# fp32 scores of 64 rows, and a recurrence whose products all span 128 rows

## The chip, the cores and the metric

The kernel runs on one core of one Trainium2 chip. The metric is device time in microseconds: a run is timed from start to end, and the median of several runs counts. Beside that, one execution was recorded by the hardware profiler; all rows below come from it. Engines are named as the profile names them: PE is TensorE (products), PEld its weight loads, DVE VectorE, ACT ScalarE, POOL GpSimd, SP the engine whose queue issues the transfers.

## The reference

One inference step of a two-layer decoder: 1024 prompt tokens and 8 single-token samples, model width 1024. In each layer one input projection feeds three branches, whose gated results go through one output projection and are added to the layer's input.

- Pooling: trailing means over 2, 4, 8 or 16 tokens, and a small product per group.
- Attention: 8 query heads and 2 key heads of 64 channels, window 128, RMS norm and rotary on queries and keys, a learned sink in the softmax.
- RWKV-7: 4 heads, each with a 64 x 64 state that goes through the tokens one after another:

```python
def step(S, inp):
    r_t, w_t, k_t, v_t, kk_t, a_t = inp
    sa = jnp.einsum('bhvk,bhk->bhv', S, kk_t)
    S = S * w_t[:, :, None, :] - sa[..., None] * (kk_t * a_t)[:, :, None, :] + v_t[..., None] * k_t[:, :, None, :]
    o = jnp.einsum('bhvk,bhk->bhv', S, r_t)
    return S, o
```

Everything is float32.

## The kernel before, in words

Activations lie with channels on partitions and tokens on columns, in two halves (512 prompt tokens and the 8 samples; 512 prompt tokens). The large projections split each float32 operand into a high and a low part (type F32R) and add three products (high by high, high by low, low by high) into one PSUM tile `acc` of 128 x 512, 128 x 256 or 128 x 264. The weight's high part `wh` is cast on ScalarE and its low part `wl` on GpSimd or VectorE; three buffers of each are in turn.

Attention works in blocks of 128 queries and a pair of query heads (`attn_block`): 32 blocks in all, 16 of a layer. The block splits its queries into `qs` (ScalarE) and `ql` (VectorE, the tile QL); the keys `kh` hold high and low parts in the two halves of the partitions, so that two F32R products over 128 rows give one score tile of 128 x 256. `e` counts the key head, `j` the query head of the pair. Each `e` has a PSUM tile `ps` of its own. Then follow the softmax in `sm`, four transposes into `pt`, the copies `pcur` and `pall`, and the product with the values into `po`.

The recurrence is chunked: 32 tokens make a chunk, eight chunks a group (`g`), four groups a layer; 64 chunks in all, strictly in order. `rwkv_prep` prepares a group: decays (`cs`, `pin`, `pc`), the scaled keys BK, the scaled queries AG, their Gram products, and the inverse of a 32 x 32 triangle per chunk and head (X, transposed into TT). Then `values` and `flip` turn the values into XS and BK into BT through the PSUM tiles CA and CB. `rwkv_chain` does a chunk in three steps. The tile XS holds per chunk, pair `p` and head `e` of the pair the state (64 partitions), the corrected keys' rows (32) and the values (32). First, four products of XS with AG give `ys`; second, TT times `ys` gives the 32 correction rows of XS; third, BT times the lower or upper 64 rows of XS is added to the decayed state and becomes the state of the next chunk. The outputs of the chunk before (`osb`) are produced between the first and the second step.

The order on TensorE is written by a planner inside the kernel: every product has a planned cost (`mm`), every operation of another engine a planned end, and each branch is a generator that gives up its turn with `yield` of the tiles it needs next. The planner puts projection products between the steps of the branches, and a dependency without a semaphore fixes the order that results. Operations within `urgent()` get a higher priority in the queues of their engines. Both PSUM tiles for scores come from a ring of two (`att`).

All VectorE, ScalarE and GpSimd operations pass line 150 and all products line 308 of the kernel before, so the rows are told apart by their tiles.

## Time and profile before

| | |
|---|---|
| median of 3 runs | 1277.89 us (1267.9 to 1283.97) |
| the profiled execution | 1278.29 us, its span 1276.5 us |
| PE busy | 1107.7 us (87%) |
| DVE busy | 985.9 us (77%) |
| ACT busy | 642.0 us (50%) |
| POOL busy | 558.3 us (44%) |
| TensorE clock granted, mean | 0.934 |

The span runs from the first instruction to the last. A busy share is the time in which the engine had at least one instruction under way. The end of a product is modelled and products overlap; where the cost of products matters, the starts of their neighbours are compared. A product with float32 operands stands in the trace as two instructions, one with F32R operands as one (the column of shapes calls both f32). A row of waits says which engine and tile waited for which, how long in total, in how many places, and the longest.

### The profile page before, as it was taken

What the parts mean: (1) busy time and instruction counts of PE and PEld (TensorE: products, weight loads), DVE (VectorE), ACT (ScalarE), POOL (GpSimd) and SP (SyncE); (2) the same over time, 40 slices, a digit from 0 to 9 for tenths busy, and PEclk for the clock granted to TensorE, in tenths of its full rate; (3) what the DMA queues carried; (4) which work ended last, traced back from release to release, by engine and by line L of the source; (5) the groups of instructions that cost most, each with busy time, mean ns of one, the idle gap of its engine ahead of it and who ended that gap; (6) DMA issues with size and microseconds to landing.
All of it is one profiled execution on the core that took longest, in us unless ns stands there. A gap on an engine that the chain in (4) does not pass through costs nothing.

```text
span 1276.5 us, 24973 instructions
## 1 busy us (share of the span) xinstructions
PE 1107.7 (87%) x9258; PEld 889.1 (70%) x9258; DVE 985.9 (77%) x2193; ACT 642.0 (50%) x1651; POOL 558.3 (44%) x535
## 2 busy tenths in 40 slices
PE   7988788699898799989998879888998886899995
PEld 6987677476665568879887767665776664588664
DVE  6487997879769887897688997989447897878633
ACT  4265445544555564763464456555535545646421
POOL 3256544633454246441545544443454462344231
PEclk8998989798899799999999979999998997899997
DMA  6522223342221124334311212434242221244221
GB/s 186 160 81 69 87 55 101 103 135 76 59 89 59 34 84 154 114 113 123 121 53 61 78 56 79 149 128 137 82 134 68 64 75 44 74 150 130 65 74 68
DMA packets 81237, 120.37 MB, mean 94 GB/s; under 512 B 20430, under 2 KB 30174, under 8 KB 81116
## 3 DMA queue, kind: packets, MB, share of 16 engines
q1 hardware_dynamic: 81116, 118.79, 29.8%
q8 instruction: 72, 1.18, 0.4%
q14 instruction: 49, 0.40, 0.1%
HBM read 94.30 MB, written 19.17 MB: 89 GB/s over the span
## 4 chain that ended last, share of the span: by engine, by line
DVE 40%; PE 37%; issue 6%; ACT 5%; DMA 5%; POOL 4%; SPq 2%; POOLq 0%; DVEq 0%; ACTq 0%
PE acc L308 26%; DVE pr L150 4%; DVE AG L150 3%; PE CA L308 3%; DVE XS L150 3%; DVE sm L150 3%; DVE asm L150 3%; DVE ql L150 2%; DVE X L150 2%; PE po L308 2%; DMA sq<-z 2%; DVE hl L150 2%; SPq L160 2%; DVE z L150 1%; PE CB L308 1%
## 5 line engine op out<-in xcount | busy, mean ns | idle before, releaser
L308 PE MATMUL acc<-hh,wh 128*128 128x512 f32 (+2 forms) x1464 | 499.7, 342 | 11.7 <-ACT hh L150 5.1
L308 PE MATMUL acc<-hh,wl 128*128 128x512 f32 (+2 forms) x1464 | 492.9, 338 | 12.5 <-POOL wl L150 9.3
L308 PE MATMUL acc<-hl,wh 128*128 128x256 f32 (+3 forms) x1464 | 494.1, 338 | 4.6 <-DVE hl L150 4.6
L150 POOL TENSOR_TENSOR wl<-wst,wh 128x512 fp32r<-128x512 f32 (+1 forms) x223 | 307.8, 1383 | 348.3 <-ACT wh L150 285.0
L308 PEld LDWEIGHTS acc<-hh,wh 128*128 128x128 f32 x1464 | 285.8, 195 | 50.4 <-issue 9.1
L308 PEld LDWEIGHTS acc<-hh,wl 128*128 128x128 f32 x1464 | 284.6, 195 | 44.7 <-POOL wl L150 12.9
L308 PEld LDWEIGHTS acc<-hl,wh 128*128 128x128 f32 (+1 forms) x1464 | 283.6, 194 | 38.0 <-issue 7.9
L150 ACT CAST wh<-wst 128x512 fp32r<-128x512 f32 (+1 forms) x246 | 149.3, 609 | 166.6 <-PE acc L308 99.9
L150 ACT ACTIVATE sm<-sm,asm 128x128 f32<-128x128 f32 (+1 forms) x130 | 50.9, 393 | 39.2 <-DVE asm L150 37.0
L150 DVE TENSOR_TENSOR pr<-X,N 128x4 f32<-128x4 f32 (+15 forms) x128 | 65.4, 511 | 2.8 <-POOL ro L150 0.9
L150 ACT CAST qs<-q 64x256 fp32r<-64x256 f32 x128 | 51.9, 405 | 22.8 <-DVE q L150 10.6
L150 ACT ACTIVATE e<-e 128x520 f32<-128x520 f32 (+1 forms) x64 | 40.5, 634 | 35.3 <-DVE e L150 34.7
L150 DVE SCALAR_TENSOR_TENSOR XS<-XS,pc,CA 64x64 f32<-64x64 f32 x128 | 35.4, 277 | 20.2 <-PE CA L308 18.5
L150 DVE TENSOR_REDUCE X<-pr 128x2 f32<-128x4 f32 (+15 forms) x128 | 44.9, 351 | 2.0
L150 POOL TENSOR_TENSOR mx<-mx,e 128x520 f32<-128x520 f32 (+1 forms) x24 | 33.7, 1404 | 28.0 <-ACT e L150 28.0
L308 PE MATMUL ps<-kh,qs 128*128 128x256 f32 (+1 forms) x128 | 37.8, 316 | 8.2 <-ACT pall L150 3.4
L311 PE MATMUL pt<-cst,sm 128*128 128x128 f32 (+1 forms) x130 | 23.8, 311 | 23.2 <-DVE sm L150 15.3
L150 POOL TENSOR_TENSOR z<-z,rope 128x520 f32<-128x520 f32 (+1 forms) x20 | 31.9, 1595 | 26.1 <-DMA sq<-z 11.2
L150 DVE SCALAR_TENSOR_TENSOR xrkv<-xrkv,vec,zl 128x256 f32<-128x256 f32 x48 | 32.9, 734 | 13.0 <-POOL xrkv L150 13.0
L150 DVE TENSOR_TENSOR ql<-q,qs 64x256 fp32r<-64x256 f32 x64 | 40.5, 632 | 2.1 <-ACT qs L150 0.9
L308 PEld LDWEIGHTS CA<-XS,BT 64*64 64x64 f32 x256 | 13.1, 139 | 39.1 <-DVE XS L150 28.6
L150 ACT ACTIVATE sa<-sa 128x512 f32<-128x512 f32 (+2 forms) x56 | 28.3, 508 | 23.9 <-POOL sa L150 11.7
(258 smaller groups left out, 2109.6 us busy)
## 6 DMA issues: line engine op xcount, KB each, us to landing
wst<-in_w_in_dram SPq DMA_DIRECT2D x175, 256.0 KB, 2.7
wst<-in_w_out_dram SPq DMA_DIRECT2D x56, 256.0 KB, 2.8
zr<-ev SPq DMA_DIRECT2D x24, 256.0 KB, 3.0
zl<-zr SPq DMA_DIRECT2D x12, 385.5 KB, 3.5
sq<-z SPq DMA_DIRECT2D x40, 65.0 KB, 2.0
sq<-z SPq DMA_DIRECT2D x40, 64.0 KB, 2.0
xh<-in_x_dram SPq DMA_DIRECT2D x8, 260.0 KB, 5.6
xr<-in_x_dram SPq DMA_DIRECT2D x8, 260.0 KB, 2.8
```

What stands on the lines that cost most here:

```text
L150: return f(*a, **kw)
L160: return nc.sync.dma_start(out, in_)
L308: placed(T.matmul(out=out, lhsT=lhsT, rhs=rhs, start=start, stop=stop, **kw), n, out)
L311: placed(T.transpose(out=out, in_=in_, identity=identity), 300 if out.shape[0] > 64 else 130, out)
```

## The change

It has two large parts and some small ones.

Scores: queries and keys are no longer split. `kh` is one float32 tile; a block has four float32 products over the 64 partitions of their head, `e` the inner loop, instead of eight over 128. Both PSUM tiles are taken before the first of them.

Recurrence: BT, TZ (which replaces TT) and XS are filled so that every product of the chain runs over all 128 partitions. BT holds an identity where the state's rows lie, written once; TZ holds each 32 x 32 inverse in its own 32 partitions and zeros elsewhere. The keys are scaled to the end of the chunk instead of its start, so the state in XS is kept already times the chunk's decay; the third step's product then gives the new state whole, and one write per half multiplies it by the next chunk's decay (ScalarE for the upper 64 partitions, VectorE for the lower). All of the chain but the outputs now uses CA.

Small: constants are laid out anew, three masks as bytes; the products of BK with `pc` are gone, a subtraction on GpSimd precedes the exponentials; half of BT's copies go to VectorE; the planner's cost for a product of up to 64 rows and more than 64 output rows is lower.

```diff
     def load_cst():
+        for to, at, n in ((0, C_ID, 256), (K_MC, C_MC, 128), (K_REC, C_REC, 30), (K_TI, C_TI, 4)):
+            D.dma_start(cst[:, to:to + n], src[:, at:at + n])
...
+        G.tensor_copy(out=masks, in_=t[:, 0:384])
...
         def decays(p, sig):
-            tt(G, sig, cs, sig, ALU.subtract)
-            act(sig, sig, AF.Exp, scale=-CD)
             pin = t2("pin")
-            act(pin, cs, AF.Exp, scale=CD)
-            act(cs, cs, AF.Exp, scale=-CD)
-            S.copy(out=R.pc[:, p, :], in_=cs[:, 31:256:32])
+            tt(G, ch8(pin), ch8(cs), ch8(cs)[:, :, 31:32].to_broadcast([128, 8, 32]), ALU.subtract)
+            act(R.pc[:, p, :], cs[:, 31:256:32], AF.Exp, scale=-CD)
+            tt(G, sig, pin, sig, ALU.subtract)
+            act(cs, pin, AF.Exp, scale=-CD)
+            act(pin, pin, AF.Exp, scale=CD)
+            act(sig, sig, AF.Exp, scale=-CD)
...
-        for p in range(2):
-            tt(
-                G, BK[:, :, p].rearrange("p c x s -> p c (x s)"), BK[:, :, p].rearrange("p c x s -> p c (x s)"),
-                R.pc[:, p, :].unsqueeze(2).to_broadcast([128, 8, 64]), ALU.mult,
-            )
...
         values(0)
         values(1)
+        for h in range(4):
+            rows = slice(32 * h, 32 * h + 32)
+            V.transpose(
+                out=TZ[rows, :, h, :].rearrange("p c (i q) -> p i c q", q=4),
+                in_=X[rows].rearrange("p i (c q) -> p i c q", q=4),
+            )
...
-            S.copy(out=BT[:, 4 * b:4 * b + 4], in_=ps)
+            for e in range(2):
+                rows = slice(64 * (1 - e), 64 * (1 - e) + 64)
+                (V.tensor_copy if e else S.copy)(out=BT[rows, 4 * b:4 * b + 4, :, e, :], in_=ps[rows])
...
             for p, e in heads:
-                mm(
-                    out=CE[p][r0:r0 + 32, 64:128], lhsT=TT[32 * h:32 * h + 32, c].rearrange("p i q -> p (i q)"),
-                    rhs=ys[32 * h:32 * h + 32, :], start=True, stop=True,
-                )
+                mm(out=upd[r0:r0 + 32, p, :], lhsT=TZ[:, c, 2 * p + e, :], rhs=ys, start=True, stop=True)
             with urgent():
-                for p, e in heads:
-                    r0 = 64 * (1 - e)
-                    (V.tensor_copy if e else S.copy)(out=XS[r0:r0 + 32, c, p, e, :], in_=CE[p][r0:r0 + 32, 64:128])
+                V.tensor_copy(out=XS[64:96, c, :, 0, :], in_=upd[64:96])
+                S.copy(out=XS[0:32, c, :, 1, :], in_=upd[0:32])
             yield (XS,)
-                    mm(
-                        out=CE[p][rows, 128:192], lhsT=BT[other, c, p, :], rhs=XS[other, c, p, e, :],
-                        start=True, stop=True,
...
-                        V.scalar_tensor_tensor(
-                            out=XS[rows, (c + 1) % 8, p, e, :], in0=XS[rows, c, p, e, :], scalar=pc[rows, p, c:c + 1],
-                            in1=CE[p][rows, 128:192], op0=ALU.mult, op1=ALU.add,
-                        )
+            for p, e in heads:
+                mm(out=new[halves[e], p, :], lhsT=BT[:, c, p, e, :], rhs=XS[:, c, p, e, :], start=True, stop=True)
+            with urgent():
+                if c < 7:
+                    for p in range(2):
+                        act(XS[halves[1], to, p, 1, :], new[halves[1], p, :], AF.Copy, scale=pc[halves[1], p, to:to + 1])
+                    tt(
+                        V, XS[halves[0], to, :, 0, :], new[halves[0]], pc[halves[0], :, to:to + 1].to_broadcast([64, 2, 64]),
+                        ALU.mult,
                     )
...
     def attn_block(L, q, att, i, jp, mixed, after):
-            S.copy(out=qs[rows, e], in_=part)
-            tt(V, QL[rows, e], part, qs[rows, e], ALU.subtract)
-            S.copy(out=qs[other, e], in_=part)
-        yield qs, QL
+        yield L.kh, q
+        ps = []
         for e in range(2):
+            yield from vacant("att")
+            ps.append(attp("ps").rearrange("p (j b k) -> p j b k", j=2, b=2))
-                mm(out=o, lhsT=qs[:, e, j, :], rhs=L.kh[:, e, cols], start=True, stop=False)
-                mm(out=o, lhsT=QL[:, e, j, :], rhs=L.kh[:, e, cols], start=False, stop=True)
+        for j in range(2):
+            for e in range(2):
+                rows = slice(64 * e, 64 * e + 64)
+                mm(
+                    out=ps[e][:, j, lo:, :].rearrange("p b k -> p (b k)"), lhsT=q[rows, 2 * jp + j, q0:q0 + 128],
+                    rhs=L.kh[rows, q0 + 128 * lo:q0 + 256], start=True, stop=True,
+                )
```

The planner writes a new order for every engine. Three places of it follow, the first two in the last group of the second layer. First VectorE, one chunk from the state's write to the correction rows, before:

```order
L150 SCALAR_TENSOR_TENSOR XS<-XS,pc,CA 64x64 [waits DVE_49,PE_49]
L150 SCALAR_TENSOR_TENSOR XS<-XS,pc,CA 64x64 [waits DVE_49]
L150 SCALAR_TENSOR_TENSOR XS<-XS,pc,CB 64x64 [waits DVE_49,PE_49]
L150 SCALAR_TENSOR_TENSOR XS<-XS,pc,CB 64x64 [waits DVE_49]
L150 COPY ys<-CA 128x64 [waits PE_49]
L150 TENSOR_TENSOR spare<-acc,spare 128x512 [waits DMAHW2_49,PE_49]
L150 COPY XS<-CA 32x64 [waits Activation_49]
L150 COPY XS<-CB 32x64 [waits Activation_49]
```

and the same engine and place with the change:

```order
L157 TENSOR_TENSOR XS<-CA,pc 64x2x64 [waits PE_49,Activation_49]
L157 COPY ys<-CA 128x64 [waits DVE_49,PE_49]
L157 TENSOR_TENSOR xr<-acc,xr 128x512 [waits PE_49]
L157 COPY XS<-CA 32x2x64 [waits PE_49]
L157 TENSOR_TENSOR XS<-CA,pc 64x2x64 [waits PE_49,Activation_49]
```

Four state operations have become one, which waits for ScalarE too; two copies into XS have become one, which no longer waits for ScalarE.

Second ScalarE in the last group, before (`osb` is the chunk's output, `wst` the weights as they come from memory):

```order
L150 CAST wh<-wst 128x512 [waits DMAHW6_49,DMAHW7_49,PE_49,Pool_49]
L150 CAST wh<-wst 128x512 [waits DMAHW0_49,DMAHW1_49,PE_49,Pool_49]
L150 COPY osb<-CB 128x64 [waits DVE_49,PE_49]
L150 COPY XS<-CA 32x64 [waits DVE_49,PE_49]
L150 COPY XS<-CB 32x64 [waits PE_49]
```

and with the change:

```order
L157 COPY osb<-CB 128x64 [waits PE_49]
L157 CAST wh<-wst 128x512 [waits DMAHW0_49,PE_49,Pool_49]
L157 COPY XS<-CA 32x2x64 [waits DVE_49]
L157 CAST wh<-wst 128x256 [waits DMAHW1_49,PE_49,Pool_49]
L157 ACTIVATE XS<-CA,pc 64x64 [waits PE_49]
L157 ACTIVATE XS<-CA,pc 64x64
```

ScalarE has one copy into XS, which waits for VectorE's, and two state writes; here a weight cast with a wait for TensorE stands between them, as in 29 of the 64 chunks.

Third TensorE, one block's scores, before (the second half of the heads follows two projection products later):

```order
L308 MATMUL ps<-kh,qs 128x256 [waits Activation_49]
L308 MATMUL ps<-kh,ql 128x256
L308 MATMUL ps<-kh,qs 128x256
L308 MATMUL ps<-kh,ql 128x256
L308 MATMUL acc<-hh,wh 128x512
L308 MATMUL acc<-hl,wh 128x512
L308 MATMUL ps<-kh,qs 128x256 [waits PE_49,Activation_49]
```

and one block with the change:

```order
L329 MATMUL acc<-hh,wh 128x256
L329 MATMUL ps<-kh,q 128x256 [waits PE_49] x2
L329 MATMUL ps<-kh,q 128x256 [waits DVE_49]
L329 MATMUL ps<-kh,q 128x256
L329 MATMUL acc<-hl,wh 128x256
```

Eight products in two runs have become four in one.

## Rows read from the trace of the kernel before

**Rows 1.** The page: span; busy us (share of the span) xinstructions of each engine.

```profile
span 1276.5 us, 24973 instructions
PE 1107.7 (87%) x9258; PEld 889.1 (70%) x9258; DVE 985.9 (77%) x2193; ACT 642.0 (50%) x1651; POOL 558.3 (44%) x535
```

**Rows 2.** Windows 100:200, 400:600, 700:750, 800:900, 1000:1050: busy us, all instructions.

```profile
sum 500.00, PE 430.04 PEld 351.80 DVE 445.44 ACT 264.30 POOL 235.13; mean PE 86.01 PEld 70.36 DVE 89.09 ACT 52.86 POOL 47.03
```

**Rows 3.** The same windows, instructions with the tile ql alone.

```profile
sum 500.00, PE 21.56 PEld 15.98 DVE 25.12 POOL 0.00; mean PE 4.31 PEld 3.20 DVE 5.02 POOL 0.00
```

**Rows 4.** The same windows, instructions with the tile XS alone.

```profile
sum 500.00, PE 22.47 PEld 13.95 DVE 30.67 ACT 13.05 POOL 0.40; mean PE 4.49 PEld 2.79 DVE 6.13 ACT 2.61 POOL 0.08
```

**Rows 5.** Waits: waiting engine and tile, releaser; us in total, places, longest us.

```profile
ACT wh L150 <- PE acc L308: 99.9, 74, 4.6
...
PE CA L308 <- DVE XS L150: 25.1, 27, 3.8
...
DVE XS L150 <- ACT XS L150: 23.2, 17, 2.8
...
PE CA L308 <- DVE ys L150: 17.0, 16, 3.5
```

**Rows 6.** VectorE by line and form: out<-in, shapes xcount | busy us, mean ns | idle before.

```profile
L150 DVE TENSOR_TENSOR ql<-q,qs 64x256 fp32r<-64x256 f32 x64 | 40.5, 632 | 2.1 <-ACT qs L150 0.9
...
L150 DVE SCALAR_TENSOR_TENSOR XS<-XS,pc,CA 64x64 f32<-64x64 f32 x128 | 35.4, 277 | 20.2 <-PE CA L308 18.5
...
L150 DVE TENSOR_TENSOR mx<-po,mx 128x128 f32<-128x128 f32 x64 | 15.7, 283 | 15.7 <-PE po L308 15.5
...
L150 DVE COPY XS<-CA 32x64 f32<-32x64 f32 x64 | 13.2, 206 | 23.5 <-ACT XS L150 22.9
...
L150 DVE STREAM_TRANSPOSE TT<-X 128x256 f32<-128x256 f32 x8 | 3.5, 436 | 0.1
...
L150 DVE COPY vt<-vtr 128x512 f32<-128x512 f32 x4 | 2.7, 683 | 1.0 <-PE vtr L311 0.9
```

**Rows 7.** TensorE's timeline, four places: start us, us, rows*columns, shape, xcount.

```profile
190.94 1.04 PE L308 MATMUL qn<-sq,cst 128*128 128x256 f32 x4
...
191.94 0.28 PE L308 MATMUL acc<-hh,wh 128*128 128x256 f32 x1
...
401.87 0.24 PE L308 MATMUL CA<-ys,TT 32*32 32x64 f32 x2
...
402.11 0.50 PE L308 MATMUL acc<-hh,wh 128*128 128x512 f32 x1
...
406.59 0.33 PE L308 MATMUL CA<-XS,BT 64*64 64x64 f32 x4
...
406.97 0.39 PE L308 MATMUL ps<-kh,qs 128*128 128x256 f32 x1
...
407.79 0.39 PE L308 MATMUL acc<-hh,wl 128*128 128x512 f32 x1
408.02 0.28 PE L308 MATMUL ps<-kh,qs 128*128 128x256 f32 x1
...
408.49 0.40 PE L308 MATMUL acc<-hh,wh 128*128 128x512 f32 x1
...
476.25 0.40 PE L308 MATMUL acc<-hh,wh 128*128 128x512 f32 x1
476.58 0.66 PE L308 MATMUL po<-pall,vt 128*64 128x256 f32 x4
...
477.94 0.39 PE L308 MATMUL acc<-hh,wl 128*128 128x512 f32 x1
478.17 0.39 PE L308 MATMUL acc<-hh,wh 128*128 128x512 f32 x1
```

**Rows 8.** ScalarE by line and form, columns as in rows 6.

```profile
L150 ACT CAST wh<-wst 128x512 fp32r<-128x512 f32 x235 | 144.9, 619 | 152.3 <-PE acc L308 88.1 <-DMA wst<-in_w_in_dram 22.1 <-issue 14.7
...
L150 ACT ACTIVATE sa<-lora,vd 128x8 f32<-128x8 f32 x8 | 1.7, 264 | 0.1
```

More of the change, by code (lines that the diff above doesn't have):

```diff
@@ L12 @@
 I32 = mybir.dt.int32
+U8 = mybir.dt.uint8
 AF = mybir.ActivationFunctionType
@@ L58 @@
 C_END = 932
+K_MP = 256
+K_MC = 257
+K_REC = 385
+K_TI = 415
+K_END = 419
 V_G = 0
@@ L189, in hybrid_step_kernel @@
     )
-    cst = sb.tile([128, C_END], F32, name="cst")
+    cst = sb.tile([128, K_END], F32, name="cst")
+    masks = sb.tile([128, 384], U8, name="masks")
     vec = sb.tile([128, 2, V_END], F32, name="vec")
@@ L304, in mm @@
             m = out.shape[0]
-            n = max(4.2 * n, 500) if m > 64 else max(2.7 * n, 235) if m > 32 else max(1.6 * n + 64, 140)
+            half = m > 64 and lhsT.shape[0] <= 64
+            n = max((2.7 if half else 4.2) * n, 500) if m > 64 else max(2.7 * n, 235) if m > 32 else max(1.6 * n + 64, 140)
         else:
@@ L805, in rwkv_chain @@
         o0 = 256 * (g % 2)
-        AG, BT, TT, pc = R.AG, R.BT, R.TT, R.pc
+        AG, pc = R.AG, R.pc
         osb = sb.tile([128, 8, 64], F32, tag="osb", name="osb")
-        if g == 0:
-            for e in range(2):
-                rows = slice(64 * e, 64 * e + 64)
+        halves = (slice(0, 64), slice(64, 128))
+        for e in range(2):
+            rows = halves[e]
+            if g == 0:
                 G.memset(XS[rows, 0, :, e, :], 0.0)
-        CE = (CA, CB)
+            else:
+                tt(
+                    (V, G)[e], XS[rows, 0, :, e, :], XS[rows, 0, :, e, :],
+                    pc[rows, :, 0:1].to_broadcast([64, 2, 64]), ALU.mult,
+                )
         heads = [(p, e) for p in range(2) for e in range(2)]
+        upd = CA[:, 64:192].rearrange("p (h v) -> p h v", h=2)
+        new = CA[:, 192:320].rearrange("p (h v) -> p h v", h=2)
         def outputs(c):
@@ new lines, in rwkv_chain @@
+            to = (c + 1) % 8
+            apart[0] = XS.tensor.name
+            with urgent():
+                if c < 7:
+                    for p in range(2):
+                        act(XS[halves[1], to, p, 1, :], new[halves[1], p, :], AF.Copy, scale=pc[halves[1], p, to:to + 1])
+                    tt(
+                        V, XS[halves[0], to, :, 0, :], new[halves[0]], pc[halves[0], :, to:to + 1].to_broadcast([64, 2, 64]),
+                        ALU.mult,
+                    )
+                else:
+                    S.copy(out=XS[halves[1], 0, :, 1, :], in_=new[halves[1]])
+                    V.tensor_copy(out=XS[halves[0], 0, :, 0, :], in_=new[halves[0]])
@@ L861, in rwkv_chain @@
+            apart[0] = None
             yield (XS,)
@@ L1020, in put @@
             if H == 0:
-                L.kh = sb.tile([128, 2, 640], F32R, tag="kh", name="kh")
+                L.kh = sb.tile([128, 640], F32, tag="kh", name="kh")
             else:
-                V.tensor_copy(out=L.kh[:, :, 0:128], in_=L.kh[:, :, 512:640])
-            tt(V, z, z, sw, ALU.add)
-            for e in range(2):
-                rows = slice(64 * e, 64 * e + 64)
-                other = slice(64 * (1 - e), 64 * (1 - e) + 64)
-                S.copy(out=L.kh[rows, e, 128:640], in_=z[rows, :HALF])
-                tt(V, L.kh[other, e, 128:640], z[rows, :HALF], L.kh[rows, e, 128:640], ALU.subtract)
+                V.tensor_copy(out=L.kh[:, 0:128], in_=L.kh[:, 512:640])
+            tt(V, L.kh[:, 128:640], z[:, :HALF], sw[:, :HALF], ALU.add)
             if H == 0:
                 L.knew = sb.tile([128, 8], F32, tag="knew", name="knew")
-                V.tensor_copy(out=L.knew, in_=z[:, HALF:])
+                tt(V, L.knew, z[:, HALF:], sw[:, HALF:], ALU.add)
             else:
-                D.dma_start(O["k_p"][L.l], z[:, 384:512])
+                D.dma_start(O["k_p"][L.l], L.kh[:, 512:640])
         return put
```

78 lines of the change are left out of this document (33 added, 45 removed).

## The prediction

> **What bounds the kernel now.** I read the page's busy shares first. TensorE is busy 1107.7 us (87%) and VectorE 985.9 us (77%) of a span of 1276.5 us [rows 1]: neither is full over the whole span, so the stretches decide. Cut into windows, five stretches of together 500 us have VectorE at 445.4 us, 89%, and TensorE at 430.0 us [rows 2]: there TensorE stands idle for 70 us while VectorE hardly stops. The view of waits says the same from TensorE's side: the steps of the recurrence wait 25.1 us for VectorE's writes of XS and 17.0 us for those of ys [rows 5]. TensorE takes its instructions in a written order, so each late VectorE result holds up the projections behind it. The reader is to see a kernel that TensorE alone would fill to 87%, and whose other 13% is mostly lateness of VectorE.
>
> The sum is made against the profiled execution, 1278.3 us; it lies 0.4 us above the median of the three runs (1277.9).
>
> **VectorE.** Gone are 64 splits of the query (ql, 632 ns each, 40.5 us); 256 state updates (half from CA, half from CB; 277 ns each by CA's row, 71 us); 128 narrow copies into XS (206 ns by CA's row, 26 us); 8 transposes TT (436 ns, 3.5 us) [rows 6]. Together 141 us. New are 64 copies and 64 state writes of 128 columns out of PSUM; the nearest row, 128 columns out of PSUM into mx, takes 283 ns: 36 us. Each of the eight groups has two copies of 512 columns into BT; vt, the same out of PSUM, takes 683 ns: 11 us. The 32 narrow transposes TZ have the 256 columns of a TT and a quarter of its partitions; between a quarter of 436 ns and all of it I take all, since the other rows of this group go with the columns (283 ns for 128, 683 for 512): 14 us, at least 3.5 [rows 6]. The first state of a group times its decay is six more of 283 ns: 2 us. Together 63 us. The key's split and the key's new sum are taken as equal. **VectorE's work falls by 78 us**, 8% of it.
>
> What that is worth depends on the place. The dense stretches hold 25.1 us of ql [rows 3] and 30.7 us of work on XS [rows 4], 55.8 of the 138 us of these kinds, two fifths; so two fifths of 78, 31 us, come off there. VectorE sets the pace for 89% of those stretches, and TensorE has 70 us of idle time to give back: 0.89 of 31, 28 us. The other 47 us come off where VectorE is busy (985.9 - 445.4) / 776.5, or 70%, of the time; work taken off there returns only where a result was late, and I choose a third, 16 us. **Sum: -44 us**; its ends are 0, if the waits only change their name, and -78.
>
> **TensorE.** Scores: the four split products of one half of the heads put 0.47 us between their neighbours (407.79 to 408.49, less the 0.23 from one projection product to the next, 477.94 to 478.17), so a block's eight cost 0.94 us [rows 7]. The four fp32 products in their place have 64 rows and 128 columns; this form stands nowhere in the trace. The nearest row has a block's four fp32 products of the same 256 moving columns, each on half of the array's columns: 476.25 to 477.94, less twice 0.23, is 1.23 us. On the whole array two such products (qn; an fp32 product stands as two instructions) took 190.94 to 191.94 less 0.12, half of 0.23 for half the columns, so 0.44 each, and four would be 1.76; the halves therefore ran beside each other (0.88), with 0.35 lost around them [rows 7]. If row halves do as column halves do, a block costs 1.23 us, 0.29 more; 32 blocks, +9 us. If they go in turn, 1.76 and 0.35, +37 us. If nothing is lost around them, 0.88, -2 us. I take +9: the row is nearest in all but the direction of the halving, and the halves write to different score tiles.
>
> The Trainium skill, in "TensorEngine Tiling (Array Packing)", section "Tiling Modes", lists two independent tiles of 64 rows by 128 columns and says that a change of mode drains the engine; by it a block is the pair price with the loss around it, and the sum stays. No row here shows that form.
>
> Inverse: the four products on 32 rows and 32 columns occupy 0.24 us (401.87 to 402.11); with all 128 rows they use two of the four column quarters, so two pairs run one after the other, as the state product's two pairs do now: 0.38 us (406.59 to 406.97) [rows 7]. 64 steps by 0.14: +9 us. The state product keeps two pairs of 64 columns: 0, between 0 and another 9, as its rows grow from 64 to 128. TensorE's work grows by 18 us; at its busy share of 87% this is **+16 us**.
>
> **ScalarE and the rest.** 128 casts of the query go, 112 state writes with a scale come, each no less than the 264 ns of a short one with an operand per partition [rows 8], 30 us. Its copies into XS halve in number and double in width. The engine is left a little lighter, and I count that at 0. GpSimd trades 16 products of BK with pc for 16 smaller subtractions ahead of the exponentials: 0, hidden since a group's preparation runs ahead of its chain; uncovered, a group would start one GpSimd operation later. SP's queue has seven transfers of constants for one, ahead of the loads for the low-rank weights, the rotary tables and the second half's input; GpSimd casts the masks and fills the identity once. The first projections cover these; I allow 1 us. The transposes TZ now follow the previous group's chain; beside them TensorE turns the values and BK in the same gap: 0, and 7 by 4 by 0.436, 12 us, if uncovered.
>
> **The bare chain.** Where no projection covers it, in the last three chunks, a state write of four VectorE operations in line (4 by 0.277, 1.1 us [rows 6]) becomes two on ScalarE and then one on VectorE (2 by 0.264 and 0.283, 0.8 us [rows 6, 8]); they are not side by side, since in the built order VectorE's half waits for ScalarE's. 0.3 by three: -1 us.
>
> **Sum:** 1278.3 - 44 + 16 + 1 - 1 = **1250 us**, own range 1230 to 1270. A faster clock where TensorE waits less is not counted.
>
> **The rivals.** *Relief in full.* In a queue that is 89% full, 8% less work may undo more lateness than it is long. For it: 70 us of idle TensorE in the dense stretches [rows 2]. Against: three fifths of the relief lie outside them. All 78 come back: 1278 - 78 + 16 = 1216. Chance 0.2.
>
> *Row halves in turn.* The scores cost +37 instead of +9; TensorE grows by 46 us, 40 at its busy share: 1278 - 44 + 40 = 1274. For it: no 64-row, 128-column form in the trace. Against: column halves do run beside each other [rows 7]. Chance 0.15.
>
> *The waits only move.* The planner writes TensorE's whole order anew; if new lateness takes the place of the old, no relief is left and 16 are paid: 1294. For it: the attention and pooling work of the dense stretches stays. Against: VectorE really has 78 us less. Chance 0.08.
>
> *ScalarE holds the chain (slower).* Before, a state update asked VectorE alone; now its upper half asks ScalarE first, and VectorE waits for that. In the built order a weight cast stands between the XS copy and the state write on ScalarE in 29 of the 64 chunks, and waits for TensorE to release a buffer. Such casts now wait for projections 99.9 us in 74 places [rows 5] and take 619 ns [rows 8]. VectorE's present waits for ScalarE's XS copy, 23.2 us in 17 places, 1.4 each [rows 5], price a held state write: 29 by 1.4 is 40 us, and with the chain late VectorE's relief finds no taker; I leave a third of it, 15: 1278 - 15 + 16 + 40 = 1319. It decides from about 20 of the 29 chunks on, where 28 us undo the forecast's gain. Against: where the cast is released before the product ends, nothing is held. Chance 0.12.
>
> The Trainium skill, in "TensorE: Matmul & The Clock Gate", section "Architectural detail: the array is 16× 32×32, not 1× 128×128", says that ScalarE and VectorE take their queues strictly in order, which this rival needs; the 17 waits agree with it.
>
> **Numbers.** My own sum has a chance of 0.45. The range is 1210 to 1294: below it lies a full relief with some help, above it most of ScalarE's case. With 2% (1252 and 1303 against 1277.9; about what a measurement of this kernel can tell from no change): faster 0.2 from full relief and a little over half of 0.45, 0.45 together; slower 0.1 from ScalarE's case and 0.02 from the moved waits, 0.12; within, the rest, 0.43.
>
> **What would show it.** VectorE busy near 908 us; score products starting in pairs at about 1.2 us a block; TensorE's waits for XS and ys together under their present 42 us. Wrong would be score products in single file, or waits for XS that name ScalarE and exceed 42 us. The forecast falls as a whole if TensorE's idle time stays near 169 us although VectorE is 78 us lighter.

## The result, and the profile after

The changed kernel takes 1268.9 us (median), the kernel before 1277.6 us beside it on the same chips. The ratio is 0.9924, with a 95% interval of 0.9903 to 0.9944: 10 us faster, between 7 and 12, which is under 1% and clear of the noise. One of the 20 executions of the changed kernel took 1984.7 us, was slow, and is left out of the ratio; the other 19 lie between 1260.9 and 1272.1. The forecast was 28 us faster (1250 against 1278.3). The sign is right, the time lies inside the range, and two thirds of the expected gain are missing.

The page of the changed kernel, as in [rows 1]:

```profile
span 1267.8 us, 24585 instructions
PE 1110.5 (88%) x9258; PEld 883.4 (70%) x9258; DVE 916.6 (72%) x1912; ACT 606.8 (48%) x1571; POOL 555.5 (44%) x543
```

VectorE is 69 us lighter and ScalarE 35, and TensorE has the same busy time as before. But TensorE's idle time (span less busy) only fell from 168.8 to 157.3 us. Relief was delivered, and little of it was taken up. The waits, as in [rows 5], show who is late now:

```profile
PE ssum L329 <- POOL pr L157: 16.5, 2, 9.2
PE CA L329 <- ACT XS L157: 14.7, 15, 2.1
PE CA L329 <- DVE XS L157: 14.0, 14, 2.9
...
PE CA L329 <- DVE ys L157: 9.1, 7, 3.4
```

```profile
ACT wh L157 <- PE acc L329: 115.1, 87, 4.4
...
ACT XS L157 <- DVE XS L157: 33.7, 24, 2.8
```

```profile
DVE XS L157 <- ACT XS L157: 21.1, 19, 2.7
```

TensorE's waits for the recurrence sum to 37.8 us (14.7, 14.0 and 9.1) where they were 42.1, and half of the XS share now names ScalarE. Behind that stands a pair of rows: ScalarE waits 33.7 us for VectorE's writes of XS, and VectorE 21.1 us for ScalarE's. The first is new. A row like the second was there before, 23.2 us [rows 5], but for another step: VectorE's copies of the inverse waited for ScalarE's. Now ScalarE waits in the inverse and VectorE in the state, once each in every chunk. I call such a wait a hand-off.

The costs of the new instructions, by line and form as in [rows 6, 8], first VectorE, then ScalarE:

```profile
L157 DVE COPY XS<-CA 32x128 f32<-32x128 f32 x64 | 18.5, 289 | 27.3 <-PE CA L329 25.9
...
L157 DVE TENSOR_TENSOR XS<-CA,pc 64x128 f32<-64x128 f32 x56 | 15.5, 276 | 18.6 <-ACT XS L157 18.0 <-PE acc L329 0.3
...
L157 DVE STREAM_TRANSPOSE TZ<-X 32x256 f32<-32x256 f32 x32 | 13.9, 434 | 0.5
```

```profile
L157 ACT ACTIVATE XS<-CA,pc 64x64 f32<-64x64 f32 x112 | 28.6, 303 | 23.7 <-PE CA L329 22.8
...
L157 ACT COPY XS<-CA 32x128 f32<-32x128 f32 x64 | 16.0, 250 | 34.4 <-DVE XS L157 33.7
```

The prices of the forecast hold: 289 and 276 ns where 283 was taken, 434 where 436, 303 above the bound of 264. What the forecast did not price is the last column: in all 64 chunks ScalarE's copy (250 ns) begins only when VectorE's (289 ns) has ended, and VectorE's state write (276 ns) only when both of ScalarE's (303 ns each) have. One chunk near the end, from the timeline (start us, us, then the wait in brackets):

```profile
1235.22 0.29 DVE L157 COPY XS<-CA 32x128 f32<-32x128 f32 x1 [0.74 <-PE CA L329]
1235.55 0.25 ACT L157 COPY XS<-CA 32x128 f32<-32x128 f32 x1 [0.86 <-DVE XS L157]
...
1235.86 0.69 PE L329 MATMUL CA<-XS,BT 128*64 128x64 f32 x8 [0.68 <-ACT XS L157]
1236.62 0.51 ACT L157 ACTIVATE XS<-CA,pc 64x64 f32<-64x64 f32 x2 [0.82 <-PE CA L329]
1237.17 0.28 DVE L157 TENSOR_TENSOR XS<-CA,pc 64x128 f32<-64x128 f32 x1 [1.65 <-ACT XS L157]
```

Read the starts: 1235.22 and 1235.55, then 1236.62 and 1237.17. The two engines write different rows of XS from different rows of CA, and go in single file. Both engines read one PSUM tile, CA, and the built program here lets the second read it only after the first.

TensorE's part came as forecast. A score block between projections, and the four products of an inverse (eight instructions):

```profile
273.53 0.40 PE L329 MATMUL acc<-hh,wl 128*128 128x512 f32 x1
273.86 1.13 PE L329 MATMUL ps<-kh,q 64*128 64x256 f32 x8
274.92 0.51 PE L329 MATMUL acc<-hh,wh 128*128 128x512 f32 x1
...
407.37 0.42 PE L329 MATMUL CA<-ys,TZ 128*32 128x64 f32 x8 [0.40 <-DVE ys L157]
407.71 0.50 PE L329 MATMUL acc<-hh,wh 128*128 128x512 f32 x1
```

From 273.53 to 274.92, less the 0.23 of one projection product, is 1.16 us a block, where 1.23 was forecast and 1.76 and more would have been the price in turn: the row halves run side by side. The inverse takes 0.34 us to the next product (forecast 0.38, before 0.24 [rows 7]).

### The profile page after: what moved, and what is told of

It reads as the page before. It is cut to its first block, busy times and chain, and to the rows that moved or that the text cites. A ratio compares the mean times of both kernels' runs of the same rounds, so it can differ in the third digit from the quotient of the medians.

```text
span 1267.8 us, 24585 instructions
## 1 busy us (share of the span) xinstructions
PE 1110.5 (88%) x9258; PEld 883.4 (70%) x9258; DVE 916.6 (72%) x1912; ACT 606.8 (48%) x1571; POOL 555.5 (44%) x543
## 5 line engine op out<-in xcount | busy, mean ns | idle before, releaser
L157 POOL TENSOR_TENSOR wl<-wst,wh 128x512 fp32r<-128x512 f32 (+1 forms) x223 | 300.6, 1350 | 396.3 <-ACT wh L157 342.3
L157 ACT ACTIVATE e<-e 128x520 f32<-128x520 f32 (+1 forms) x64 | 40.5, 633 | 39.2 <-DVE e L157 38.4
L157 ACT COPY XS<-CA 32x128 f32<-32x128 f32 (+2 forms) x88 | 27.3, 311 | 50.0 <-DVE XS L157 33.7
L329 PE MATMUL ps<-kh,q 64*128 64x256 f32 (+1 forms) x256 | 41.0, 412 | 6.6 <-ACT pall L157 3.6
L329 PEld LDWEIGHTS CA<-XS,BT 128*64 128x64 f32 x512 | 21.3, 144 | 33.5 <-ACT XS L157 20.3
L157 DVE COPY XS<-CA 32x128 f32<-32x128 f32 (+1 forms) x72 | 20.7, 287 | 30.6 <-PE CA L329 25.9
L329 PE MATMUL CA<-XS,BT 128*64 128x64 f32 x512 | 30.4, 243 | 13.5 <-ACT XS L157 13.4
L157 DVE TENSOR_TENSOR ev<-acc,ss 128x256 f32<-128x256 f32 (+2 forms) x36 | 18.4, 512 | 31.3 <-PE acc L329 22.8
L157 DVE SCALAR_TENSOR_TENSOR hl<-xh,vec,hh 128x520 fp32r<-128x520 f32 (+1 forms) x32 | 30.8, 972 | 14.0 <-ACT hh L157 13.8
```

The lines of the kernel that those rows point to most:

```text
L157: return f(*a, **kw)
L329: placed(T.matmul(out=out, lhsT=lhsT, rhs=rhs, start=start, stop=stop, **kw), n, out)
```

## The experiments

Theory A: VectorE's relief finds little taker. Theory B: the relief is worth what the forecast said, and the hand-offs between ScalarE and VectorE eat it. Theory C: TensorE's newly written order eats it. A run's time is the median of 4 to 12 executions, and each ratio is against runs of the kernel before made beside it; in us it is taken off 1277.

| run | ratio | interval | against before, us |
|---|---|---|---|
| the change | 0.9924 | 0.9903 to 0.9944 | -10 |
| e1 without ql | 0.9844 | 0.9805 to 0.9883 | -20 |
| e2 scores alone | 0.9830 | 0.9796 to 0.9865 | -22 |
| e3 two PSUM tiles | 0.9771 | 0.9743 to 0.9799 | -29 |
| e4 all on VectorE | 0.9770 | 0.9740 to 0.9799 | -29 |
| e5 inverse in two tiles | 0.9877 | 0.9841 to 0.9912 | -16 |
| e6 state in two tiles | 0.9835 | 0.9796 to 0.9874 | -21 |
| e7 old recurrence, by pair | 0.9849 | 0.9812 to 0.9887 | -19 |
| e8 e3, sums later | 0.9787 | 0.9752 to 0.9822 | -27 |
| e9 e1, fewer casts | 0.9825 | 0.9784 to 0.9865 | -22 |
| e10 e3, scores twice | 1.0053 | 1.0021 to 1.0084 | +7 |
| e11 e3, waits back | 0.9899 | 0.9862 to 0.9935 | -13 |
| e12 e3, BT in two tiles | 0.9907 | 0.9873 to 0.9940 | -12 |

**e1: is VectorE's relief worth anything?** The planner still counts the subtraction, so TensorE's order stays the same row for row; the instruction isn't issued, and QL is zero.

```diff
-            tt(V, QL[rows, e], part, qs[rows, e], ALU.subtract)
+            V.eng = skip
+            tt(V, QL[rows, e], part, qs[rows, e], ALU.subtract)
+            V.eng = nc.vector
```

> The kernel before, without the 64 subtractions that make the low part of the query (ql, 632 ns each on VectorE): the low part is zero, so the scores lack that term. TensorE's written order and all other work stay as they are; VectorE alone is 40.5 us lighter. Forecast's own rule (relief is worth 0.89 in the dense stretches, where 25.1 us of it lie, and a third elsewhere, 15.4 us): 22 + 5 = 27 us faster than before, 1250. Theory A, VectorE's relief finds little taker because the next late result stands right behind it: at most 10 us faster (a quarter of 40.5), 1268 to 1278. Theory B, the relief is worth what the forecast said and the new hand-offs between ScalarE and VectorE in the recurrence eat it: 20 to 30 us faster, as the forecast. Theory C, the newly written order of TensorE eats it: 20 to 30 us faster too, since the order here is the old one.

Measured: 20 us faster than before (15 to 25), for 40.5 us less work on VectorE. A falls: relief is worth about a half of its length here, somewhat less than the forecast's rule (27).

**e2: the scores alone.** The kernel before with the parts of the change in `k_dst` and `attn_block`, without QL and with the planner's new price; the recurrence is the old one.

```diff
-                mm(out=o, lhsT=qs[:, e, j, :], rhs=L.kh[:, e, cols], start=True, stop=False)
-                mm(out=o, lhsT=QL[:, e, j, :], rhs=L.kh[:, e, cols], start=False, stop=True)
...
+                    out=ps[e][:, j, lo:, :].rearrange("p b k -> p (b k)"), lhsT=q[rows, 2 * jp + j, q0:q0 + 128],
+                    rhs=L.kh[rows, q0 + 128 * lo:q0 + 256], start=True, stop=True,
```

> The kernel before with the fp32 scores of 64 rows alone; the recurrence is the old one. VectorE loses 40.5 us (ql), ScalarE 128 casts, TensorE gains 32 blocks by 0.32, 10 us, and the order is planned anew. Theory A (little taker): 9 us dearer by TensorE, at most 10 us back: within 5 us of before. Theory B (hand-offs of the new recurrence eat the relief; none of them is here): 20 to 27 us of relief less 9: 11 to 18 us faster than before, so faster than the whole change. Theory C (a new order is a draw of its own): anywhere from 15 us faster to 10 us slower.

Measured: 22 us faster than before, which is 12 faster than the whole change. That is also more than any of the three theories had expected, though the interval (17 to 26) reaches into B's 11 to 18. So the rest of the change, the recurrence with its small parts and the order planned for them, made the kernel slower by about 12 us as it was built. B reads it so, and C could too, since e2 has a new order of its own. The TensorE work that the scores add doesn't show within the interval.

**e3: the hand-offs taken away.** The same instructions on every engine, in the same order on TensorE (in four spots of the trace a projection product stands a few places elsewhere); only the place of the products in PSUM differs.

```diff
-        upd = CA[:, 64:192].rearrange("p (h v) -> p h v", h=2)
-        new = CA[:, 192:320].rearrange("p (h v) -> p h v", h=2)
+        upd = [t[:, 64:192].rearrange("p (h v) -> p h v", h=2) for t in (CA, CB)]
+        new = [t[:, 320:448].rearrange("p (h v) -> p h v", h=2) for t in (CA, CB)]
...
-                mm(out=new[halves[e], p, :], lhsT=BT[:, c, p, e, :], rhs=XS[:, c, p, e, :], start=True, stop=True)
+                mm(out=new[e][halves[e], p, :], lhsT=BT[:, c, p, e, :], rhs=XS[:, c, p, e, :], start=True, stop=True)
```

> The changed kernel with the two row halves of the inverse's and the state's products in two PSUM tiles (CA and CB) in place of one. The same instructions in the same order on TensorE; what goes is the wait of ScalarE's copy for VectorE's in the inverse's write and of VectorE's state write for ScalarE's two, 64 of each: the built order shows both without it. Theory A: 0 to 5 us faster than the changed kernel (1264 to 1269). Theory B: 15 to 25 us faster than it (1244 to 1254). Theory C: as A, since the order stays.

Measured: 1247.5 us, 29 us faster than before and 20 us faster than the changed kernel (0.9771 against 0.9924). B's forecast holds: taking the hand-offs away gives back 20 us. A's and C's for this run (0 to 5 us) fall; the order is the same, so it isn't what held these 20 us. Whether the new order costs something beside them, e3 can't tell. The page and the waits of this run:

```profile
span 1247.1 us, 24550 instructions
PE 1106.9 (89%) x9258; PEld 879.5 (71%) x9258; DVE 920.8 (74%) x1912; ACT 607.4 (49%) x1571; POOL 554.4 (44%) x543
```

```profile
PE ssum L329 <- POOL pr L157: 13.2, 2, 8.4
PE CA L329 <- DVE XS L157: 11.9, 15, 2.3
...
PE CA L329 <- DVE ys L157: 10.1, 10, 3.4
...
PE CA L329 <- ACT XS L157: 2.7, 2, 1.7
```

TensorE's waits for the recurrence are now 24.7 us (37.8 in the changed kernel), its idle time is 140 us (157), and neither of the two rows between ScalarE and VectorE is left. A chunk in the same place of the program:

```profile
1214.79 0.29 DVE L157 COPY XS<-CA 32x128 f32<-32x128 f32 x1 [0.50 <-PE CA L329]
1214.89 0.26 ACT L157 COPY XS<-CB 32x128 f32<-32x128 f32 x1 [0.50 <-PE CB L329]
...
1215.62 0.28 DVE L157 TENSOR_TENSOR XS<-CA,pc 64x128 f32<-64x128 f32 x1 [0.54 <-PE CA L329]
1215.68 0.51 ACT L157 ACTIVATE XS<-CB,pc 64x64 f32<-64x64 f32 x2 [0.54 <-PE CB L329]
```

Now both begin as soon as the product is there (1214.79 and 1214.89; 1215.62 and 1215.68), and both name PE in their brackets.

**e4: one engine for all writes.** The other way to have no hand-off.

```diff
-                S.copy(out=XS[0:32, c, :, 1, :], in_=upd[0:32])
+                V.tensor_copy(out=XS[0:32, c, :, 1, :], in_=upd[0:32])
...
-                    for p in range(2):
-                        act(XS[halves[1], to, p, 1, :], new[halves[1], p, :], AF.Copy, scale=pc[halves[1], p, to:to + 1])
-                    tt(
-                        V, XS[halves[0], to, :, 0, :], new[halves[0]], pc[halves[0], :, to:to + 1].to_broadcast([64, 2, 64]),
-                        ALU.mult,
-                    )
+                    for e in range(2):
+                        tt(
+                            V, XS[halves[e], to, :, e, :], new[halves[e]], pc[halves[e], :, to:to + 1].to_broadcast([64, 2, 64]),
+                            ALU.mult,
+                        )
```

> The changed kernel with all writes of the recurrence into XS (the inverse's two, the state's two) on VectorE: no hand-off is left, ScalarE loses 64 copies of 250 ns and 112 state writes of 303 ns (50 us), VectorE gains 64 copies and 64 state writes of 283 ns (36 us). Theory A (VectorE's work is worth at most a quarter of its length): 0 to 9 us slower than the changed kernel, 1269 to 1278. Theory B (hand-offs cost 15 to 25 us; 36 us of VectorE's work cost 18 to 20): about level with the changed kernel, 1264 to 1274, and 15 to 25 us below what VectorE's load alone would give. Theory C: a new order again, 10 us either way.

Measured: 1247.0 us, 20 us faster than the changed kernel, although VectorE is 32 us busier (948.8 against 916.6). A's sign is wrong, and B, which had the hand-offs' gain used up by the added VectorE work, expected level: both miss. That the added work cost nothing can't be read from this run alone. ScalarE is 45 us lighter here (561.9 against 606.8), and TensorE's order was planned anew: some two fifths of its rows stand elsewhere.

**e5 and e6: which hand-off?** e3's edit for the inverse alone, and for the state alone.

Edits, e5 first, then e6 (the matching operands of the products and of the writes change with them):

```diff
-        upd = CA[:, 64:192].rearrange("p (h v) -> p h v", h=2)
+        upd = [t[:, 64:192].rearrange("p (h v) -> p h v", h=2) for t in (CA, CB)]
```

```diff
-        new = CA[:, 192:320].rearrange("p (h v) -> p h v", h=2)
+        new = [t[:, 320:448].rearrange("p (h v) -> p h v", h=2) for t in (CA, CB)]
```

> The changed kernel with two PSUM tiles for the inverse's product alone; the state's product keeps one tile. Of the two hand-offs of a chunk, ScalarE's copy no longer waits for VectorE's, and VectorE's state write still waits for ScalarE's two. Both gone were worth 21 us (1268 to 1247). If each of the 128 hand-offs costs alike: half, 10 us faster than the changed kernel, 1258. If the cost goes with the work that now stands in line (0.25 us of copy in the inverse, 0.28 us of VectorE's write in the state): 10 too. If it goes with the idle time that the changed kernel's waits show (ScalarE for VectorE's copy 33.7 us, VectorE for ScalarE's writes 21.1 us): 13 us, 1255. If the state's hand-off is all of it: 0, 1268.

> The changed kernel with two PSUM tiles for the state's product alone; the inverse's product keeps one tile. Alike or by work in line: 10 us faster than the changed kernel, 1258. By the idle time of the waits: 8 us, 1260. If the state's hand-off is all of it: 1247.

Measured against the changed kernel: 6 us faster without the inverse's hand-off (0.9877), 11 without the state's (0.9835); together 17, and 20 when both go (e3). The state's looks the dearer one: in the changed kernel its second engine waits for two writes of 303 ns, the inverse's for one of 289. But the two intervals overlap, and e5's touches the changed kernel's, so this order isn't settled. The guess by the idle time of the waits (13 and 8) seems to have it the wrong way round.

**e11: is it the wait itself?** e3's tiles, with the two waits put back by hand between instructions that now read different tiles.

```diff
-                V.tensor_copy(out=XS[64:96, c, :, 0, :], in_=upd[0][64:96])
-                S.copy(out=XS[0:32, c, :, 1, :], in_=upd[1][0:32])
+                one = V.tensor_copy(out=XS[64:96, c, :, 0, :], in_=upd[0][64:96])
+                behind(S.copy(out=XS[0:32, c, :, 1, :], in_=upd[1][0:32]), one)
```

> The version with two PSUM tiles, and the waits put back by hand: ScalarE's inverse copy waits for VectorE's, and VectorE's state write for ScalarE's last, although they read different tiles. If the waits were the loss: 21 us slower than that version, 1268, as the changed kernel. If it was the reading of one tile by two engines, and not the wait: 1247.

Measured: 16 us slower than e3 (0.9899 against 0.9771), most of the 20; the interval overlaps that of the changed kernel, so the other 4 us are within the noise. TensorE's waits for VectorE's XS go from 11.9 back to 25.6 us, its idle time from 140 to 157 us, and both rows between the two engines are back:

```profile
PE CA L335 <- DVE XS L157: 25.6, 25, 2.9
```

```profile
ACT XS L157 <- DVE XS L157: 43.3, 33, 3.8
```

```profile
DVE XS L157 <- ACT XS L157: 20.3, 19, 2.7
```

So the wait is the cost, and not how two engines read one tile. From the traces, the time from the modelled end of a step's four products (eight instructions) to the end of its last write into XS, mean over the 64 chunks, in us:

| | inverse | state |
|---|---|---|
| before | 2.41 | 2.24 |
| the change | 2.03 | 2.05 |
| e3 | 1.49 | 1.53 |
| e5 (state still in line) | 1.48 | 2.20 |
| e6 (inverse still in line) | 2.01 | 1.51 |
| e11 | 1.82 | 2.13 |
| e4 | 2.05 | 1.64 |
| e2 | 2.55 | 2.31 |
| e7 | 1.63 | 2.31 |

Each hand-off adds about half a microsecond of delay to its step: 0.54 us in the inverse and 0.52 in the state, change less e3, by 64 chunks is 68 us of delay. 20 us of it are time; the rest lies beside projections. The 20 us are not spread evenly: by the starts of the chunks in the two traces, the changed kernel's lag on e3 stays between 5.4 and 5.8 us from the 17th chunk to the 26th, and is 17.6 us at the 49th.

The length of a step's delay alone doesn't set the time. e4's inverse is as late as the changed kernel's, and e4 is as fast as e3. And e2, with the old recurrence, has later writes than the change in both steps (2.55 and 2.31 us against 2.03 and 2.05) and is still 12 us faster. TensorE's waits for the recurrence are shorter in the change than in e2 (37.8 us against 43.2, which are rows of 28.7, 4.5 and 10.0); its other idle time is longer (119.5 us against 104.4). So e3 and e11 show what the hand-offs cost in the changed kernel. They don't show that the hand-offs alone put it behind e2; the order planned anew (C) may have a part in that, and this stays open.

**e7: does every hand-off cost?** e2's kernel; the four copies of the old inverse are dealt to the engines by tile and not by half.

```diff
-                    (V.tensor_copy if e else S.copy)(out=XS[r0:r0 + 32, c, p, e, :], in_=CE[p][r0:r0 + 32, 64:128])
+                    (V.tensor_copy if p else S.copy)(out=XS[r0:r0 + 32, c, p, e, :], in_=CE[p][r0:r0 + 32, 64:128])
```

> The kernel with the fp32 scores alone (the second run of this study), its old recurrence kept, but of the four inverse copies of a chunk ScalarE takes the two out of CA and VectorE the two out of CB, where each engine took one out of either. The same number of copies on each engine; the 128 waits of VectorE's copies for ScalarE's are gone from the built order, apart from 25. If a hand-off costs 0.16 us (21 us by 128) wherever it stands: 64 chunks by 0.16, 10 us faster than that run, 1246. If the old hand-off was hidden (VectorE had been busy until then anyway): level with it, 1253 to 1259.

Measured: level with e2 (0.9849 and 0.9830, intervals overlapping). The hand-off did go: the inverse's delay fell from 2.55 to 1.63 us a chunk, and TensorE's waits for XS from 33.2 to 19.5 us in these rows of e2 and of e7:

```profile
PE CA L306 <- DVE XS L150: 28.7, 24, 3.1
...
PE CB L306 <- DVE XS L150: 4.5, 4, 2.6
```

```profile
PE CB L306 <- DVE XS L150: 12.7, 10, 2.5
...
PE CA L306 <- DVE XS L150: 6.8, 5, 2.3
```

Yet TensorE's idle time stays (147.6 and 144.5 us), and its busy time rises by 4.6, at a granted clock of 0.931 where e2 has 0.936. A price for each hand-off, carried over from e3, misses here: this one cost nothing that shows. TensorE's order was also planned anew in this run; whether the hand-off was hidden or the new order took its gain stays open.

**e8: the longest single wait.** e3, with TensorE's row of waits for `ssum` (13.2 us in two places) moved.

```diff
             tt(G, pr, ss, bc(0), ALU.mult)
             yield (pr,)
+            yield 6.0
```

> The version with two PSUM tiles for both products, and the third sum of the sample's state (ssum after pr) placed 6 us later in TensorE's order. In that version TensorE waits for it 13.2 us in two places. If those waits are lost time: 8 to 13 us faster than it, 1234 to 1239. If the next late result stands right behind: level, 1245 to 1250. A newly written order may add or take some us of its own.

Measured: level with e3 (0.9787). The wait went, and others of its size stand in the list of this run that are not among e3's longest. One is at another product of the same chain of sums: the second sum of the second pair, 6.5 us in the first layer, where e3 has no wait.

```profile
PE pool L329 <- DVE pd L157: 12.0, 3, 7.1
PE ssum L329 <- DVE pr L157: 10.4, 2, 6.5
```

A wait at the head of the list is not its length in time. For theory C this is one sample: another order of the same work moved the time by 2 us, within the intervals.

**e9: is ScalarE's relief worth anything?** e1 without the second cast of the query.

```diff
-            S.copy(out=qs[other, e], in_=part)
+            S.eng = skip
+            S.copy(out=qs[other, e], in_=part)
+            S.eng = nc.scalar
```

> The kernel before without the subtractions ql (as in the first run of this study) and without the 64 casts of the query into the other rows (qs, 405 ns each on ScalarE, 26 us), so the scores lack the products with the key's low part too. TensorE's order as before. The forecast's step, ScalarE's relief is worth 0: level with the first run, 1252 to 1259. If ScalarE's work is worth what VectorE's was (20 us for 40.5, about a half): 13 us faster than it, 1243.

Measured: level with e1 (0.9825 and 0.9844), with ScalarE at 614.0 us where e1 has 640.7. Half of its length, 13 us, is outside the intervals. ScalarE's load is worth nothing that shows, as the forecast counted it; its place in the chain is another matter.

**e10: what does added TensorE work cost?** e3, each score product issued twice; the planner counts the second at nothing.

```diff
+                for again in range(2):
+                    mm(
...
+                        rhs=L.kh[rows, q0 + 128 * lo:q0 + 256], start=True, stop=True, free=again,
+                    )
```

> The version with two PSUM tiles, with every fp32 score product issued twice in a row (the second gives the same result), the order otherwise kept. A block's eight instructions measured 1.26 us in the changed kernel, so TensorE does 32 by about 1.2, 38 us more. By the forecast's rule (added TensorE work times its busy share, 87%): 33 us slower than that version, 1281. If TensorE's added work fills its own waiting time, half of it: 19 us, 1266. If it also lowers the granted clock or delays the recurrence: 45 us or more, from 1292 up.

Measured: 36 us slower than e3 (1.0053 against 0.9771; 28 to 44 by the ends of the intervals). A block with its products doubled, between projections:

```profile
273.52 0.40 PE L329 MATMUL acc<-hh,wl 128*128 128x512 f32 x1
273.85 2.10 PE L329 MATMUL ps<-kh,q 64*128 64x256 f32 x16
275.88 0.51 PE L329 MATMUL acc<-hh,wh 128*128 128x512 f32 x1
```

From 273.52 to 275.88, less 0.23, is 2.13 us where the single block takes 1.16: 0.97 more, about 30 us for 32 blocks of which four are narrower (not the 38 that the expectation had). Added work on TensorE comes out at about its length or somewhat more; the forecast's 0.87 of it, 26 us, lies just under the interval.

**e12: more of the same.** If two tiles help the chain, then perhaps the restart of a group as well.

```diff
-            ps = (CA, CB)[b].rearrange("p (c h v) -> p c h v", c=4, h=2)
+            ps = [(CA, CB)[b ^ e].rearrange("p (c h v) -> p c h v", c=4, h=2) for e in range(2)]
...
-                        flip(ps[r0:r0 + 64, c, p, :], BK[rows, 4 * b + c, p].rearrange("p x s -> p (x s)"), rows)
+                        flip(ps[e][r0:r0 + 64, c, p, :], BK[rows, 4 * b + c, p].rearrange("p x s -> p (x s)"), rows)
...
-                (V.tensor_copy if e else S.copy)(out=BT[rows, 4 * b:4 * b + 4, :, e, :], in_=ps[rows])
+                (V.tensor_copy if e else S.copy)(out=BT[rows, 4 * b:4 * b + 4, :, e, :], in_=ps[e][rows])
```

> The version with two PSUM tiles, and at each group's start the flipped BK by row halves in two tiles as well, so that VectorE's two copies of 512 columns into BT no longer wait for ScalarE's; that wait shows 6.4 us in 9 places in that version. If these copies are on the chain's path: 4 to 8 us faster than it, 1240 to 1243. If the restart of a group is covered by projections: level, 1245 to 1250.

Measured: 17 us slower than e3 (0.9907 against 0.9771), a miss of both expectations. The first line of TensorE's waits in this run is new, and the timeline of the first group shows what it is:

```profile
PE CB L329 <- DVE BT L157: 15.7, 8, 4.4
```

```profile
202.00 0.58 ACT L157 COPY BT<-CA 64x512 f32<-64x512 f32 x1
...
202.35 0.68 DVE L157 COPY BT<-CB 64x512 f32<-64x512 f32 x1
...
203.08 0.27 PE L329 MATMUL CB<-cst,BK 64*64 64x64 f32 x1 [1.74 <-DVE BT L157]
```

In e3 the first half of the flips uses CA and the second CB, so TensorE fills one while the other is copied out. With both halves in both tiles TensorE stands until both copies have ended, eight times, 15.7 us in all, close to the 17 us lost. The two tiles were a double buffer already, and using them for the engines took them from TensorE.

## Why the prediction was right and wrong

**VectorE, -44: near.** Its busy time fell by 69 us where the sum had 78 of work (the last section shows why the two differ). e1 priced 40.5 us of relief at 20 us, where the rule had 27; at e1's rate 78 us are 38. The choice between its ends, 0 and -78, was sound.

**TensorE, +16: near.** 1.16 us a block and 0.34 us an inverse are both a little under the forecast: 0.22 and 0.10 more than before, 13 us of work where the sum had 18. e10 shows that added score products come out at about their length; in the change itself this term wasn't isolated, and e2 shows nothing of it. *Row halves in turn* is out: that would have been 1.76 us and more. The form of two 64-row tiles that the prediction quoted the Trainium skill for ("TensorEngine Tiling (Array Packing)", "Tiling Modes") now has a row, and it agrees that the tiles are independent; what a change of mode costs, no row shows by itself.

**ScalarE, 0, and the bare chain, -1: the step that failed.** The prediction's words are: "The engine is left a little lighter, and I count that at 0." As a load that is right (e9). But the change had put ScalarE into the chain, and the prediction knew how: "they are not side by side, since in the built order VectorE's half waits for ScalarE's." That fact it priced in three chunks, as *The bare chain*, with a gain of 0.3 us each, and nowhere else. The wait stands in all 64 chunks, and a second one, of ScalarE for VectorE's inverse copy, which the section on the change names, got no price at all. Together they are worth 20 us (e3), 16 of them come back with the waits alone (e11), and with them out the kernel takes 1247.5 us, where 1250 was forecast. So the term that was put at nothing is as large as the gap: -44 + 16 was 28 us, the change without its hand-offs has 29, with them 10. That 28 and 29 agree so closely is in part luck: with the prices measured here, 38 for VectorE's relief and 13 for TensorE's work, the sum is 25, and e3's interval is 26 to 33. That the time of the change still lies inside the stated range owes nothing to the reasoning: the range was wide enough to hold it without the hand-offs.

The bare chunks themselves show it too, though they are a small part of it: e3 gains 2.6 of its 20 us there. From one chunk's first product on XS to the next's it was 3.11 us before (1238.09 to 1241.20), 3.76 in the changed kernel (1233.75 to 1237.51) and 2.30 in e3 (1213.65 to 1215.95). A second effect is in the 3.76: the granted clock in that stretch is 0.51, the lower of its levels, and 1.00 in the other two. TensorE was busy for 1.99 of 4.00 us there; the eight instructions of its state products took 0.69 us (above), and 0.45 at 410.89, amid projections. Over the whole span the clock is 0.934 before, 0.935 after and 0.943 in e3, and with it goes that e3 has the same TensorE work in 3.6 us less busy time.

**The slower rival** had the right place, VectorE behind ScalarE, and the wrong mechanism and price: 40 us from weight casts that stand ahead in ScalarE's queue. In e3 as many casts go through the same queue, and it is the fastest version together with e4. Its sign (waits for XS that name ScalarE and exceed 42 us) did not come: TensorE shows 14.7. The waits to look at were those between ScalarE and VectorE, 33.7 and 21.1 us, and the row for them was already there in [rows 5], 23.2 us in the old inverse, used only as a price.

**The sign of failure** was well chosen: TensorE's idle time near 169 us although VectorE is lighter. It fell by 12 us only, to 157.

The Trainium skill, in "PSUM — Partial Sum Buffer", section "PSUM bank collisions raise a hardware error", says that two engines may use one bank at the same time in different groups of 32 partitions, and that accesses have to be kept apart by bank and such group. The four writes here read rows 64 to 95 beside 0 to 31, and 0 to 63 beside 64 to 127. By that rule none of the 128 waits is needed; the built program guards the whole tile. A run with both engines reading one tile at once was not tried; e3 gets there by a second tile.

## What to carry to other kernels

When a change deals one step's output to two engines, look in the built order whether the second waits for the first, and ask for the price of that wait at every place where the step occurs, not only where nothing covers it. The price differs from place to place: 20 us for the 128 waits here, nothing that shows for e7's. Two engines that drain one PSUM tile go in single file here. A second tile gave 20 us back with the same instructions, and one engine for both writes gave as much, with another order of TensorE; a second tile that was the double buffer of the engine that fills it cost 17 us instead (e12). A price per microsecond is best measured before the sum is made. Instructions left out with the order kept gave about 0.5 for VectorE and nothing that shows for ScalarE; products added on TensorE cost about 1.

## What the runs showed of the hardware that was not expected

Leaving out 40.5 us of VectorE's work (e1) lowered its busy time by 25.8 us only (985.9 to 960.1): other instructions grew, by 13.0 us in sum over the forms that both traces have alike. One kind is the low half of the input (hl, 128 x 512), 849 ns in the mean before and 1009 in e1. Two of its rows in the kernel before, the second with GpSimd's instruction beside it:

```profile
230.85 0.74 DVE L150 SCALAR_TENSOR_TENSOR hl<-xh,vec,hh 128x512 fp32r<-128x512 f32 x1
```

```profile
876.06 1.53 POOL L150 TENSOR_TENSOR ss<-ss,sq 128x512 f32<-128x512 f32 x1 [0.87 <-ACT sq L150]
...
876.69 1.45 DVE L150 SCALAR_TENSOR_TENSOR hl<-xh,vec,hh 128x512 fp32r<-128x512 f32 x1
```

Alone it takes 0.74 us, and 1.45 where a GpSimd instruction ran during the first 0.90 of it. The Trainium skill, in "SBUF — State Buffer", section "Who interferes with whom", says that the two share a pair of ports under an exclusive lock, which the first to issue holds for its whole instruction, and that a VectorE instruction with two inputs in SBUF contends for it. By it, an estimate, the instruction would need 0.90 and 0.74, 1.64 us; it took 1.45, so the rows agree with a lock in kind and not quite in size. What the size is, the trace shows: this kernel has three instructions of this kind over 1.3 us (1.80, 1.70 and 1.45); each began while a GpSimd instruction ran (for another 1.24, 1.15 and 0.91 us), and each ended 0.55 or 0.56 us after that one did. So about 0.2 of its 0.74 us seem to be done while it stands. A microsecond of work taken off VectorE is thus not a microsecond off its busy time: what moves up may now run beside GpSimd and take longer there. That this accounts for all of the missing 14.7 us was not tried.
